# Gate and up products of a feed-forward net: one 512-column matmul for both parts of the input

## The chip, the cores and the metric

One Trainium2 chip; the program runs on 1 of its NeuronCores. The metric is the device time of one execution in microseconds (us), less is better. In the tables PE is TensorE (PEld is its loading of the stationary operand), DVE is VectorE, ACT is ScalarE, POOL is GpSimd and SP is SyncE, which here only issues DMAs.

## What is computed

Two transformer blocks, one after the other, on 256 tokens of width 1024, in float32. Between them lie six feed-forward nets of the same form (two in the first block, four in the second), two mixed attention layers, a stick-breaking attention and a sliding-window attention. Only the feed-forward nets are touched:

```python
# first block, for each of 2 layers:
h = rms_norm(x, ffn_norm[l])
x = x + (jax.nn.silu(h @ w_gate[l]) * (h @ w_up[l])) @ w_down[l]
# second block, four times:
x = x + 0.5 * swiglu(rms_norm_2(x, gain), w_gate_up, w_down)
def swiglu(h, w_gate_up, w_down):
    gate, up = jnp.split(h @ w_gate_up, 2, axis=-1)
    return (jax.nn.silu(gate) * up) @ w_down
```

The hidden width is 2816, which is 22 blocks of 128.

## The kernel before

**Float32 out of two parts.** Every operand of a large product is split into a high part, rounded to the matmul's input format, and a low part, the rest. A product is three matmuls into one PSUM region (`mm3`, lines 397 to 400): high by high (L398), then the two mixed ones (L399, L400). Low by low is left out.

**Weights.** All weights stream from HBM in units of up to 128 x 1024. SP issues a unit's DMA into one of 5 `raw` buffers; ACT copies it to the high part `wh` (L224) and DVE subtracts to get the low part `wl` (L225). There are 8 pairs of `wh` and `wl`. `free` (L246) drops a unit after its last use and calls `pump` (L242), which splits further units until 6 are alive. So a split stands in ACT's and DVE's order right behind the product that freed a unit, and ahead of whatever the program writes next. Each engine runs its instructions in the order in which they are written; the program is recorded in source order and nothing reorders it.

**A feed-forward net** (`ffn`, L499). The normed input lies transposed in `hh` and `hl` (high and low part, each 128 x 2 token tiles x 8 x 128). Hidden blocks 0 and 1 are made first, in another form with tokens as rows (two PSUM banks `gu`, two tiles `sgs` of the tag `sg`). Then the loop over f = 2 to 21 makes one hidden block each, with tokens as columns: gate into the left half of a PSUM bank (`gemm_a`, 8 steps k of three 256-column matmuls), up into the right half, then Silu (L543), the multiplication (L544), and the split into `ah` and `al` (`hilo`, L487 and L488). In each pass the down product of block f-2 follows (`rows_steps`, 12 matmuls of 512 columns into `o`), so `ah` and `al` have two passes of time. Passes 2, 20 and 21 have no down product, and pass 3 has those of blocks 0 and 1.

**Pass 3** holds one more thing: between its gate and its up product the tiles `sgs` of blocks 0 and 1 are transposed on PE into the bank `aT` (L528) and split by `hilo`; its down products need that result at the end of the same pass. The tag `sg` has two buffers, both held by `sgs` until those transposes have read them:

```python
            sg = wk.tile([128, 256], F32, name="sg", tag="sg", bufs=2)
            ACT.activation(out=sg, in_=ps[:, 0:256], func=AF.Silu)
            DVE.tensor_tensor(out=sg, in0=ps[:, 256:512], in1=sg, op=ALU.mult)
            acts[f] = act_tiles()
            hilo(sg, *acts[f])
```

So the Silu of pass 2 (and the one of pass 3) can't be written to `sg` before these transposes.

**PSUM.** `gbank` deals out four banks for `gu`, `tp` and `aT`; four others hold the down product.

Of the kernel before, what the change touches and what calls it, by code (L numbers as in the profile page):

```python
# [10 lines left out]
F32 = mybir.dt.float32  # L11
F32R = mybir.dt.float32r
BF16 = mybir.dt.bfloat16
I32 = mybir.dt.int32
AF = mybir.ActivationFunctionType
ALU = mybir.AluOpType
# [160 lines left out]
def kernel(ctx: ExitStack, tc: tile.TileContext, x_in, wst, gains, rows, pos, rpb, t5, cst_in, out):  # L177
    nc = tc.nc
    PE, ACT, DVE, POOL = nc.tensor, nc.scalar, nc.vector, nc.gpsimd

    pc = ctx.enter_context(tc.tile_pool(name="const", bufs=1))
    wk = ctx.enter_context(tc.tile_pool(name="work", bufs=2))
# [30 lines left out]
    def flush():  # L213
        while late:
            late.pop(0)()
# [14 lines left out]
    def ahead(n, engine=None):  # L230
        while done["split"] <= min(n, len(units) - 1):
            split_piece(done["split"], engine or DVE)
            done["split"] += 1

    def unit(key):
        n = index[key]
        ahead(n)
        if n + 1 == done["split"]:
            flush()
        return split[n]  # L240

    def pump():  # L242
        while not held[0] and len(split) < (W_BUFS if far[0] else LIVE) and done["split"] < len(units):
            ahead(done["split"])

    def free(key):  # L246
        del split[index[key]]
        pump()
# [2 lines left out]
    cst = pc.tile([128, C_END], F32, name="cst")  # L251
    row = pc.tile([128, R_END], F32, name="row")
    x = pc.tile([128, 2, D], F32, name="x")
    hh = pc.tile([128, 2, 8, 128], F32R, name="hh")
    hl = pc.tile([128, 2, 8, 128], F32R, name="hl")
    ident = cst[:, C_ID:C_ID + 128]
    zero = pc.tile([128, 1], F32, name="zero")
    mhalf = pc.tile([128, 8], F32, name="mhalf")
# [11 lines left out]
    def gbank(name):  # L270
        return pp.tile([128, 512], F32, name=name, tag="g", bufs=4)
# [100 lines left out]
    def posts(a, b):  # L372

        return {a: lambda: norm_post(1, (0,)), b: lambda: norm_post(1, (1,))}
# [22 lines left out]
    def mm3(ps, lh, ll, rh, rl, first, last):  # L397
        PE.matmul(ps, lhsT=lh, rhs=rh, start=first, stop=False)  # L398
        PE.matmul(ps, lhsT=ll, rhs=rh, start=False, stop=False)  # L399
        PE.matmul(ps, lhsT=lh, rhs=rl, start=False, stop=last)  # L400

    def gemm_a(key, ps):

        wh, wl = unit(key)
        for k in range(8):
            sl = slice(k * 128, (k + 1) * 128)
            mm3(ps, wh[:, sl], wl[:, sl], hh[:, :, k, :], hl[:, :, k, :], k == 0, k == 7)
            if k == 3:
                yield
        free(key)  # L410
        yield

    def gemm_b(keys, outs, n, nk, tiles=(0, 1), between=None):


        for i in tiles:
            for u, key in enumerate(keys):
                wh, wl = unit(key)
                for kk in range(nk):
                    k = u * nk + kk  # L420
                    sl = slice(kk * n, (kk + 1) * n)
                    if between and k in between:
                        between[k]()
                    mm3(outs[i], hh[:, i, k, :], hl[:, i, k, :], wh[:, sl], wl[:, sl], k == 0, k == 7)
                if i == 1:
                    free(key)
                yield
# [13 lines left out]
    def rows_steps(keys, acts, scale, nxt):  # L441


        banks = [[dbank("o") for _ in range(2)] for _ in range(2)]
        n = len(keys)

        def ready(c):
            while acts(c) is None:
                yield "wait"

        for c in range(n - SKEW):
            yield from ready(c)
            for i in range(2):
                rows_product(keys[c], *acts(c), banks, i, first=c == 0)
                yield
        far[0] = True
        pump()
        for c in range(n - SKEW, n - 1):
            yield from ready(c)
            rows_product(keys[c], *acts(c), banks, 0, halves=(0, 1) if c < n - 2 else (0,))  # L460
            yield
        yield from ready(n - 1)
        held[0] = True
        rows_product(keys[n - 1], *acts(n - 1), banks, 0, last=True, halves=(0,))
        residual(0, 0, banks, scale, nxt)
        rows_product(keys[n - 2], *acts(n - 2), banks, 0, halves=(1,))
        rows_product(keys[n - 1], *acts(n - 1), banks, 0, last=True, halves=(1,))
        yield
        residual(0, 1, banks, scale, nxt)
        finish(0, nxt)  # L470
        for c in range(n - SKEW, n - 2):
            rows_product(keys[c], *acts(c), banks, 1)
        rows_product(keys[n - 2], *acts(n - 2), banks, 1, halves=(0,))
        rows_product(keys[n - 1], *acts(n - 1), banks, 1, last=True, halves=(0,))
        residual(1, 0, banks, scale, nxt)
        if nxt is not None:
            norm_post(0)
        rows_product(keys[n - 2], *acts(n - 2), banks, 1, halves=(1,))
        rows_product(keys[n - 1], *acts(n - 1), banks, 1, last=True, halves=(1,))
        residual(1, 1, banks, scale, nxt)  # L480
        if nxt == 2:
            ahead(done["split"])
        finish(1, nxt)
        held[0] = far[0] = False

    def hilo(src, hi, lo):
        ACT.activation(out=hi, in_=src, func=AF.Copy)  # L487
        DVE.tensor_tensor(out=lo, in0=src, in1=hi.bitcast(F32), op=ALU.subtract)  # L488
# [5 lines left out]
    def drain(gen):  # L494
        for _ in gen:
            pass


    def ffn(tag, scale, nxt):  # L499
        if tag == ("ffn", 0):  # L500
            load_hank(1)
        acts = {}
        heads, sgs = [gbank("gu") for _ in range(2)], []
        for i in range(2):
            for part, c in (("g", 0), ("u", 256)):
                between = posts(T0, T1) if i == 0 and part == "u" else None
                drain(gemm_b([(tag, part, "head", j) for j in range(2)], {i: heads[i][:, c:c + 256]}, 256, 4, (i,), between))
            sg = wk.tile([128, 256], F32, name="sg", tag="sg", bufs=2)
            ACT.activation(out=sg, in_=heads[i][:, 0:256], func=AF.Silu)
            DVE.tensor_tensor(out=sg, in0=heads[i][:, 256:512], in1=sg, op=ALU.mult)  # L510
            sgs.append(sg)
            if i == 0:
                pump()
        order = [(tag, "d", f) for f in range(NF)]
        down = rows_steps(order, lambda c: acts.get(c), scale, nxt)

        def steps(n):
            for _ in range(n):
                next(down, None)

        for f in range(2, NF):
            ps = gbank("gu")
            drain(gemm_a((tag, "g", f), ps[:, 0:256]))
            if f == 3:
                pt = gbank("aT")
                for i in range(2):
                    for g in range(2):
                        PE.transpose(pt[:, g * 256 + i * 128:g * 256 + (i + 1) * 128], sgs[i][:, g * 128:(g + 1) * 128], ident)  # L528
                for g in range(2):
                    acts[g] = act_tiles()  # L530
                    hilo(pt[:, g * 256:(g + 1) * 256], *acts[g])
            if f == NF - 2:
                far[0] = True
            if f == 4 and settled:
                settle()
            if f == 6 and tag == ("ffn", 0):
                prepare_rope()
            if f == 12 and tag == ("ffn", 0):
                na_bias(1)
            held[0] = f == NF - 1  # L540
            drain(gemm_a((tag, "u", f), ps[:, 256:512]))
            sg = wk.tile([128, 256], F32, name="sg", tag="sg", bufs=2)
            ACT.activation(out=sg, in_=ps[:, 0:256], func=AF.Silu)  # L543
            DVE.tensor_tensor(out=sg, in0=ps[:, 256:512], in1=sg, op=ALU.mult)  # L544
            acts[f] = act_tiles()
            hilo(sg, *acts[f])
            held[0] = False
            pump()
            if 3 <= f < NF - 2:
                steps(4 if f == 3 else 2)  # L550
            acts.pop(f - 4, None)
        drain(down)
# [71 lines left out]
    def load_hank(l):  # L624

        hanks[l] = []
        for h in range(4):
            t = wk.tile([128, 6, 64], F32, name="hank", tag="cat", bufs=4)
            for rl in range(2):
                POOL.dma_start(out=t[rl * 64:(rl + 1) * 64],  # L630
                                  in_=bass.AP(rpb.tensor, rpb.offset + ((l * 4 + h) * 15 + 5 - rl) * 127,
                                              [[1, 64], [127, 6], [1, 64]]))
            hanks[l].append(t)
# [779 lines left out]
```

## Time and profile before

| | |
|---|---|
| three runs, median | 1611.92 us (1611.55 to 1612.4) |
| the profiled execution | 1613.55 us |
| its span, first to last instruction | 1611.8 us |
| mean granted TensorE clock | 0.998 |
| PE, PEld busy | 98%, 90% |
| DVE, ACT, POOL busy | 60%, 51%, 4% |
| matmuls of gate and up in the loop (256 columns) | 5760 |
| matmuls of the down products and output products (512 columns) | 1968 |

The profile is of one execution. The busy share of PE counts a matmul from its start to its modelled end, and matmuls overlap; what a matmul costs in a row of matmuls is the step from its start to the next one's. In the chain of waits the span is followed back from the last instruction, at each step to what released it; what stands there with a large share set the time. "Idle before" in the views of one engine is time in which it waited, with the instruction that ended the wait.

### The profile page before, as it was taken

What the parts mean: (1) busy time and instruction counts of PE and PEld (TensorE: products, weight loads), DVE (VectorE), ACT (ScalarE), POOL (GpSimd) and SP (SyncE); (2) the same over time, 40 slices, a digit from 0 to 9 for tenths busy, and PEclk for the clock granted to TensorE, in tenths of its full rate; (3) what the DMA queues carried; (4) which work ended last, traced back from release to release, by engine and by line L of the source; (5) the groups of instructions that cost most, each with busy time, mean ns of one, the idle gap of its engine ahead of it and who ended that gap; (6) DMA issues with size and microseconds to landing.
All of it is one profiled execution on the core that took longest, in us unless ns stands there. A gap on an engine that the chain in (4) does not pass through costs nothing.

```text
span 1611.8 us, 27684 instructions
## 1 busy us (share of the span) xinstructions
PE 1580.2 (98%) x11204; PEld 1452.2 (90%) x11204; DVE 965.8 (60%) x1619; ACT 819.4 (51%) x1405; POOL 59.1 (4%) x86
## 2 busy tenths in 40 slices
PE   7999999999999999999999999999999999999999
PEld 6888999988899998999999989999999998699998
DVE  6786655577665456755565466545655558865553
ACT  5665444457654444544447764444444446754442
POOL 1101000020000000000000000000000002000000
PEclk9999999999999999999999999999999999999999
DMA  8635555553355555465545437555456564246552
GB/s 268 217 122 164 199 199 194 176 170 119 106 174 194 194 195 171 172 220 182 185 146 195 133 104 242 180 192 198 168 196 195 179 189 131 83 152 203 182 183 75
DMA packets 79088, 279.99 MB, mean 174 GB/s; under 512 B 9072, under 2 KB 10608, under 8 KB 78960
## 3 DMA queue, kind: packets, MB, share of 16 engines
q1 hardware_dynamic: 78192, 276.64, 52.2%
q0 software_dynamic: 768, 1.57, 0.5%
q8 instruction: 88, 1.44, 0.3%
q14 instruction: 40, 0.33, 0.1%
HBM read 277.13 MB, written 1.05 MB: 173 GB/s over the span
## 4 chain that ended last, share of the span: by engine, by line
PE 90%; DVE 4%; ACT 2%; DMA 2%; issue 1%; SPq 0%; POOL 0%; DVEq 0%; ACTq 0%; POOLq 0%
PE gu L398 15%; PE gu L399 15%; PE gu L400 15%; PE o L399 9%; PE o L400 9%; PE o L398 9%; DVE wl L225 2%; PE s L801 2%; PE k L398 1%; DMA raw<-in_w_dram 1%; PE k L399 1%; PE k L400 1%; PE q L398 1%; PE v L398 1%; PE v L400 1%; PE q L399 1%
## 5 line engine op out<-in xcount | busy, mean ns | idle before, releaser
L225 DVE TENSOR_TENSOR wl<-raw,wh 128x1024 fp32r<-128x1024 f32 (+2 forms) x510 | 601.1, 1221 | 117.0 <-ACT wh L224 116.1
L398 PE MATMUL gu<-hh,wh 128*128 128x256 f32 x1920 | 540.2, 281 | 0.0
L400 PE MATMUL gu<-hl,wh 128*128 128x256 f32 x1920 | 539.4, 281 | 0.0
L399 PE MATMUL gu<-hh,wl 128*128 128x256 f32 x1920 | 538.9, 281 | 0.0
L224 ACT ACTIVATE wh<-raw 128x1024 fp32r<-128x1024 f32 (+2 forms) x510 | 506.5, 1042 | 50.3 <-DMA raw<-in_w_dram 30.1
L399 PEld LDWEIGHTS gu<-hh,wl 128*128 128x128 f32 x1920 | 361.8, 188 | 4.0
L398 PEld LDWEIGHTS gu<-hh,wh 128*128 128x128 f32 x1920 | 361.4, 188 | 4.0
L400 PEld LDWEIGHTS gu<-hl,wh 128*128 128x128 f32 x1920 | 361.6, 188 | 0.0
L543 ACT ACTIVATE sg<-gu 128x256 f32<-128x256 f32 x120 | 45.9, 383 | 434.9 <-PE gu L400 421.7
L399 PE MATMUL o<-wh,al 128*128 128x512 f32 x656 | 258.4, 394 | 3.9 <-DVE al L488 3.9
L398 PE MATMUL o<-wh,ah 128*128 128x512 f32 x656 | 259.9, 396 | 0.4 <-ACT ah L487 0.4
L400 PE MATMUL o<-wl,ah 128*128 128x512 f32 x656 | 257.7, 393 | 0.0
L544 DVE TENSOR_TENSOR sg<-gu,sg 128x256 f32<-128x256 f32 x120 | 50.9, 424 | 303.4 <-ACT sg L543 303.4
L399 PEld LDWEIGHTS o<-wh,al 128*128 128x128 f32 x656 | 123.2, 188 | 28.5 <-DVE al L488 6.3
L400 PEld LDWEIGHTS o<-wl,ah 128*128 128x128 f32 x656 | 123.1, 188 | 26.7
L398 PEld LDWEIGHTS o<-wh,ah 128*128 128x128 f32 x656 | 123.6, 188 | 25.7 <-issue 2.8
L488 DVE TENSOR_TENSOR al<-sg,ah 128x256 fp32r<-128x256 f32 x120 | 51.1, 426 | 58.0 <-ACT ah L487 58.0
L487 ACT ACTIVATE ah<-sg 128x256 fp32r<-128x256 f32 x120 | 50.1, 418 | 70.1 <-DVE sg L544 70.1
L616 ACT ACTIVATE p<-p,mn 128x256 f32<-128x256 f32 x96 | 46.1, 482 | 30.3 <-DVE mn L613 30.1
L487 ACT ACTIVATE hh<-tp 128x512 fp32r<-128x512 f32 x40 | 23.0, 598 | 64.0 <-PE tp L368 64.0
L398 PE MATMUL gu<-wh,hh 128*128 128x256 f32 x192 | 54.7, 285 | 0.0
L399 PE MATMUL gu<-wh,hl 128*128 128x256 f32 x192 | 54.1, 282 | 0.0
(242 smaller groups left out, 1892.8 us busy)
## 6 DMA issues: line engine op xcount, KB each, us to landing
raw<-in_w_dram SPq DMA_DIRECT2D x498, 512.0 KB, 4.6
gb<-in_gains_dram SPq DMA_DIRECT2D x11, 512.0 KB, 4.8
raw<-in_w_dram SPq DMA_DIRECT2D x8, 416.0 KB, 5.4
hank<-in_t_dram SPq DMA_DIRECT2D x8, 192.0 KB, 5.0
hank<-in_rpb_dram POOLq DMA_DIRECT2D x16, 96.0 KB, 5.1
out_dram<-x SPq DMA_DIRECT2D x4, 256.0 KB, 2.0
raw<-in_w_dram SPq DMA_DIRECT2D x2, 384.0 KB, 4.0
x<-in_x_dram SPq DMA_DIRECT2D x2, 256.0 KB, 3.0
```

Of the source, the lines that this page charges most:

```text
L224: ACT.activation(out=hi, in_=src, func=AF.Copy)
L225: late.append(lambda: engine.tensor_tensor(out=lo, in0=src, in1=hi.bitcast(F32), op=ALU.subtract))
L398: PE.matmul(ps, lhsT=lh, rhs=rh, start=first, stop=False)
L399: PE.matmul(ps, lhsT=ll, rhs=rh, start=False, stop=False)
L400: PE.matmul(ps, lhsT=lh, rhs=rl, start=False, stop=last)
L487: ACT.activation(out=hi, in_=src, func=AF.Copy)
L488: DVE.tensor_tensor(out=lo, in0=src, in1=hi.bitcast(F32), op=ALU.subtract)
L543: ACT.activation(out=sg, in_=ps[:, 0:256], func=AF.Silu)
L544: DVE.tensor_tensor(out=sg, in0=ps[:, 256:512], in1=sg, op=ALU.mult)
L616: ACT.activation(out=p[:, sl], in_=p[:, sl], func=AF.Exp, scale=-1.0, bias=mn[:, b:b + 1], accum_out=sm[:, b:b + 1])
L801: PE.matmul(ps[:, i * 256:(i + 1) * 256], lhsT=q[pr, i * 128:(i + 1) * 128], rhs=k[pr, :], start=True, stop=True)
```

## The change

`hh` and `hl` become two views of one tile `hx`, so that both parts of the input for one k can be streamed as one right-hand side of 4 x 128 columns. For the blocks 2 to 21, gate and up are made by a new function: per k one 512-column matmul by `wh` (left half of the bank: `wh` by `hh`; right half: `wh` by `hl`) and one 256-column matmul by `wl` into the left half. Gate and up now have a bank each. The halves are added afterwards by `whole`: ACT copies the right half to an SBUF tile `t`, DVE adds the left half to it. Silu is written after the gate's product and reads `t`; the multiplication reads `t` and `sg`.

```diff
-    hh = pc.tile([128, 2, 8, 128], F32R, name="hh")
-    hl = pc.tile([128, 2, 8, 128], F32R, name="hl")
+    hx = pc.tile([128, 4, 8, 128], F32R, name="hx")
+    hh, hl = hx[:, 0:2], hx[:, 2:4]
...
+    def gemm_wide(key, ps):
+        wh, wl = unit(key)
+        for k in range(8):
+            sl = slice(k * 128, (k + 1) * 128)
+            def high():
+                PE.matmul(ps, lhsT=wh[:, sl], rhs=hx[:, :, k, :], start=k == 0, stop=k == 7)
+            if k < 7:
+                high()
+            PE.matmul(ps[:, 0:256], lhsT=wl[:, sl], rhs=hh[:, :, k, :], start=False, stop=False)
+            if k == 7:
+                high()
+        free(key)
...
         for f in range(2, NF):
-            ps = gbank("gu")
-            drain(gemm_a((tag, "g", f), ps[:, 0:256]))
+            t = wk.tile([128, 512], F32, name="t", tag="p", bufs=5)
+            sg = wk.tile([128, 256], F32, name="sg", tag="sg", bufs=2)
+            def whole(ps, c):
+                ACT.activation(out=t[:, c:c + 256], in_=ps[:, 256:512], func=AF.Copy)
+                DVE.tensor_tensor(out=t[:, c:c + 256], in0=ps[:, 0:256], in1=t[:, c:c + 256], op=ALU.add)
+            ps = gbank("g")
+            gemm_wide((tag, "g", f), ps)
+            whole(ps, 0)
+            ACT.activation(out=sg, in_=t[:, 0:256], func=AF.Silu)
             if f == 3:
...
-            drain(gemm_a((tag, "u", f), ps[:, 256:512]))
-            sg = wk.tile([128, 256], F32, name="sg", tag="sg", bufs=2)
-            ACT.activation(out=sg, in_=ps[:, 0:256], func=AF.Silu)
-            DVE.tensor_tensor(out=sg, in0=ps[:, 256:512], in1=sg, op=ALU.mult)
+            ps = gbank("u")
+            gemm_wide((tag, "u", f), ps)
+            whole(ps, 256)
+            DVE.tensor_tensor(out=sg, in0=t[:, 256:512], in1=sg, op=ALU.mult)
```

The order in which ACT's instructions stand moves most at passes 2 and 3. These are ACT's instructions of the kernel before from the end of pass 2's gate to the transposed blocks, in the first feed-forward net of the second block's second layer (`sg_12790` is pass 2's Silu, `ah_12793` its high part, `ah_12833` and `ah_12837` are the high parts of the transposed blocks, `wh` are splits of weights):

```order
L224 ACTIVATE wh_12756<-raw_12666 128x1024
L224 ACTIVATE wh_12786<-raw_12684 128x1024
L543 ACTIVATE sg_12790<-gu_12729 128x256
L487 ACTIVATE ah_12793<-sg_12790 128x256
L224 ACTIVATE wh_12824<-raw_12702 128x1024
L487 ACTIVATE ah_12833<-aT_12828 128x256
L487 ACTIVATE ah_12837<-aT_12828 128x256
```

The Silu is the first of them that needs the transposes; three instructions stand between it and the second transposed half's. These are ACT's instructions of the changed kernel at the same place (`t_11928` is pass 2's sum, `t_11986` pass 3's, `g` and `u` the banks, `ah_12019` and `ah_12023` the transposed blocks):

```order
L224 ACTIVATE wh_11949<-raw_11865 128x1024
L543 ACTIVATE t_11928<-g_11930 128x256
L549 ACTIVATE sg_11929<-t_11928 128x256
L224 ACTIVATE wh_11975<-raw_11883 128x1024
L543 ACTIVATE t_11928<-u_11956 128x256
L504 ACTIVATE ah_11982<-sg_11929 128x256
L224 ACTIVATE wh_12007<-raw_11901 128x1024
L543 ACTIVATE t_11986<-g_11988 128x256
L549 ACTIVATE sg_11987<-t_11986 128x256
L504 ACTIVATE ah_12019<-aT_12014 128x256
L504 ACTIVATE ah_12023<-aT_12014 128x256
```

The Silu of pass 2 now stands ahead of the split `wh_11975` and of the copy of pass 2's up product, and the Silu of pass 3 with its copy ahead of the transposed blocks. PE's order at the same place, from the last matmuls of pass 3's gate to the first of its up product:

```order
L425 MATMUL g_11988<-hx_67,wl_11868 128x256 x2
L421 MATMUL g_11988<-hx_67,wh_11867 128x512
L554 MATMUL aT_12014<-cst_64,sg_11838 128x128 x2
L554 MATMUL aT_12014<-cst_64,sg_11925 128x128 x2
L421 MATMUL u_12027<-hx_67,wh_11903 128x512
L425 MATMUL u_12027<-hx_67,wl_11904 128x256
```

The transposes stand where they stood, between gate and up of pass 3; the products around them are now pairs of a 512-column and a 256-column matmul.

## Rows read from the trace of the kernel before

**Rows 1.** The page's first lines: span, and busy time of each engine.

```profile
span 1611.8 us, 27684 instructions
PE 1580.2 (98%) x11204; PEld 1452.2 (90%) x11204; DVE 965.8 (60%) x1619; ACT 819.4 (51%) x1405; POOL 59.1 (4%) x86
```

**Rows 2.** The chain of waits, shares of the span by engine.

```profile
PE 90%; DVE 4%; ACT 2%; DMA 2%; issue 1%; SPq 0%; POOL 0%; DVEq 0%; ACTq 0%; POOLq 0%
```

**Rows 3.** Groups of instructions: busy us, mean ns | idle before, releaser.

```profile
L225 DVE TENSOR_TENSOR wl<-raw,wh 128x1024 fp32r<-128x1024 f32 (+2 forms) x510 | 601.1, 1221 | 117.0 <-ACT wh L224 116.1
...
L224 ACT ACTIVATE wh<-raw 128x1024 fp32r<-128x1024 f32 (+2 forms) x510 | 506.5, 1042 | 50.3 <-DMA raw<-in_w_dram 30.1
...
L543 ACT ACTIVATE sg<-gu 128x256 f32<-128x256 f32 x120 | 45.9, 383 | 434.9 <-PE gu L400 421.7
...
L544 DVE TENSOR_TENSOR sg<-gu,sg 128x256 f32<-128x256 f32 x120 | 50.9, 424 | 303.4 <-ACT sg L543 303.4
...
L487 ACT ACTIVATE ah<-sg 128x256 fp32r<-128x256 f32 x120 | 50.1, 418 | 70.1 <-DVE sg L544 70.1
```

**Rows 4.** PE's instructions in time, one pass: start us, us, instruction.

```profile
694.28 0.28 PE L398 MATMUL gu<-hh,wh 128*128 128x256 f32 x1
...
699.96 0.40 PE L398 MATMUL o<-wh,ah 128*128 128x512 f32 x1
...
702.73 0.28 PE L398 MATMUL gu<-hh,wh 128*128 128x256 f32 x1
```

**Rows 5.** PE in time: the end of one net, then pass 3 of the next.

```profile
1132.06 0.40 PE L398 MATMUL o<-wh,ah 128*128 128x512 f32 x1
...
1164.60 0.60 PE L528 MATMUL aT<-cst,sg 128*128 128x128 f32 x4
...
1167.88 0.39 PE L398 MATMUL o<-wh,ah 128*128 128x512 f32 x1
1168.91 0.50 PE L399 MATMUL o<-wh,al 128*128 128x512 f32 x1 [0.65 <-DVE al L488]
```

**Rows 6.** ACT's instructions in time, in the same two nets.

```profile
1133.19 0.42 ACT L487 ACTIVATE ah<-sg 128x256 fp32r<-128x256 f32 x1 [0.49 <-DVE sg L544]
...
1150.76 0.38 ACT L509 ACTIVATE sg<-gu 128x256 f32<-128x256 f32 x1
1151.02 4.85 ACT L224 ACTIVATE wh<-raw 128x1024 fp32r<-128x1024 f32 x5
...
1165.02 0.38 ACT L543 ACTIVATE sg<-gu 128x256 f32<-128x256 f32 x1 [2.71 <-PE aT L528]
1165.89 0.42 ACT L487 ACTIVATE ah<-sg 128x256 fp32r<-128x256 f32 x1 [0.49 <-DVE sg L544]
1166.22 1.05 ACT L224 ACTIVATE wh<-raw 128x1024 fp32r<-128x1024 f32 x1
1167.17 0.36 ACT L487 ACTIVATE ah<-aT 128x256 fp32r<-128x256 f32 x1
```

**Rows 7.** DVE's instructions in time, pass 3 of the second.

```profile
1165.43 0.42 DVE L544 TENSOR_TENSOR sg<-gu,sg 128x256 f32<-128x256 f32 x1 [1.87 <-ACT sg L543]
...
1167.30 1.23 DVE L225 TENSOR_TENSOR wl<-raw,wh 128x1024 fp32r<-128x1024 f32 x1 [0.53 <-ACT wh L224]
1168.44 0.42 DVE L488 TENSOR_TENSOR al<-aT,ah 128x256 fp32r<-128x256 f32 x1
```

**Rows 8.** Stretches: length, busy us of five engines, granted clock, DMA, GB/s.

```profile
340.00:342.00 2.00, 2.00 (x11) 2.00 (x10) 1.26 (x7) 0.24 (x1) 0.60 (x1) 0.50 0.71 182
342.00:343.00 1.00, 1.00 (x4) 0.95 (x4) 1.00 (x4) 0.00 (x0) 0.76 (x1) 0.50 0.47 188
...
1360.00:1362.00 2.00, 0.00 (x0) 0.00 (x0) 1.35 (x4) 0.93 (x4) 1.84 (x4) 1.00 0.60 156
```

**Rows 9.** PE in time, ahead of the first of these stretches.

```profile
338.42 0.39 PE L398 MATMUL v<-wh,hh 128*128 128x256 f32 x1 [1.28 <-ACT wh L224]
...
339.68 0.38 PE L400 MATMUL v<-wl,hh 128*128 128x256 f32 x1 [0.76 <-DVE sw L705]
```

## The prediction, on record before the changed kernel ran

> **What bounds the kernel now.** I read the busy times first: PE is busy in 98% of the span, DVE in 60%, ACT in 51% [rows 1]. A busy PE alone proves nothing, since its matmuls overlap, so the chain of waits comes next: 90% of it is PE, 4% DVE, 2% ACT [rows 2]. The kernel ends when PE has worked through its list. A change is then worth what it takes out of that list, less what it makes PE wait. The price of a matmul is the step from start to start, not its duration. From 694.28 to 699.96 us stand the 48 matmuls of one pass's gate and up, 118.3 ns each; from 699.96 to 702.73 the 12 of a down product, 230.8 ns each [rows 4]. A pass takes 8.45 us, and PE waits for nothing in it. Last I looked for places where PE does wait in a feed-forward net, since other engines' work is free only away from those. There is one in each of the six nets, in pass 3: the second down matmul starts 1.03 us after the first instead of 0.23, held by the low part of the transposed blocks, a loss of 0.80 us [rows 5]. Behind it stands a chain that begins when the transposes release Silu's buffer. I priced that chain again for the new order.
>
> **PE's list.** Per step k, three 256-column matmuls (355.0 ns) become one of 512 and one of 256 columns (230.8 + 118.3 = 349.1 ns). The columns streamed are the same; what goes is one matmul's fixed share, 5.8 ns. A product of 8 steps saves 47 ns, and there are 240 of them. The up product of pass 3 saves nothing, as PE waits behind it; 234 x 0.0467 = **10.9 us** are left. The 512-column step is taken from the down products, whose right-hand side is one run of weights; no row shows a right-hand side of four runs of 128. The bounds are 0 (the wide matmul costs as much as two narrow ones) and 21.8 us: at 2.4 GHz, the level that the clock has in nearly all of the span, 256 columns are 106.7 ns, so that a narrow matmul has 11.6 ns beyond its columns, and at most those go with it. I take 5.8 because both steps are measured in the same pass. The Trainium skill (TensorE: Matmul & The Clock Gate, section "Wait — 56ns, not 53.3ns?") gives a warm step as columns over 2.4 GHz plus about 2.5 ns, for any width; by that the change would save 2.5 ns per step k, an estimate of 4.7 us in all. Both steps measured here are longer than that rule has them (109.2 and 215.8 ns), and the measured ones stand in the sum.
>
> **ACT and DVE in a common pass.** Added are two copies and two additions per pass. ACT has three splits, Silu and the high part, 3 x 1.04 + 0.38 + 0.42 = 3.9 us [rows 3]; two copies at about Silu's price make it 4.7 of 8.4 us. DVE goes from 3 x 1.22 + 2 x 0.42 = 4.5 to 5.4 us. A block's parts are needed two passes later, and a split is made six units ahead, so the new waits (ACT for the end of gate and of up, DVE for each copy) have cover: I cost them at nothing. If the cover went, each block would be late by the addition and the step to the next engine, some 0.5 us, or 60 us over 120 passes. The last block of a net has least cover. Its high part starts 1.13 us after the first of the 15 matmuls (3.46 us) that still need nothing of it [rows 5, 6]. The added copy, addition and a split of 0.95 us that now stands between them move it by about 1.4, which still fits. The gate's own bank costs nothing either: four banks go round, and each was added up a pass earlier.
>
> **Pass 3.** Silu of pass 2 writes a buffer that the transposes read. Before, it starts 0.42 us after they do (1164.60 to 1165.02), having held ACT for 2.71 us [rows 5, 6]; the parts of pass 2, one split and the transposed blocks follow. Now the same Silu stands ahead of a split and of pass 2's up copy, and the copy and Silu of pass 3's gate stand ahead of the transposed blocks. Everything between has to run after the transposes. From their start, each interval taken between two starts of [rows 5 to 7]:
>
> - Silu 0.42; split behind it 0.26 later (as 1150.76 to 1151.02): 0.68.
> - The split's low part on DVE 1.08 later, and DVE is free for the addition 1.14 after that (1166.22, 1167.30, 1168.44): 2.90. The up copy ended before, on ACT.
> - Multiplication and high part of block 2, 0.46 each (1165.43 to 1165.89): 3.82.
> - Next split 0.33 later: 4.15; its low part 1.08 later, the gate's addition 1.14 later: 6.37.
> - Silu of pass 3, 0.46: 6.83; high part of the transposed block 0.26: 7.09; low part 0.46: 7.55; PE starts 0.47 after that (1168.44 to 1168.91): **8.02 us**.
>
> Before, it was 1168.91 - 1164.60 = 4.31. So each net gets 3.71 us longer here, **22.3 us** for six. PE arrives after 3.28 (1164.60 to 1167.88) - 0.05 + 0.23 = 3.46 us and waits about 4.6. The second half follows within 0.9 us, under the eleven matmuls of the first, and no later wait comes of it: the splits that are late belong to pass 4 and the passes after it, and ACT and DVE have 3 us free per pass. DMAs start later with them, but five buffers lie ahead. Bounds: 0.8 us as now, and 10 us if the two splits also wait for their data.
>
> **The clock.** A wait of 4.6 us is longer than any in a feed-forward net before. After waits of 1.28 and 0.76 us close together [rows 9] the granted clock was 0.50, the 1.2 GHz level, from 340 to 343 us, while PE worked [rows 8]; half of such a stretch, 1.5 us, is lost. It stayed at 1.00 through 2 us without a matmul at 1360 [rows 8]. I expect one fall in each net and, since part of it may lie in the wait, 1.1 us for each: **6.6 us**, with bounds of 0 and 9. The Trainium skill (TensorE: Matmul & The Clock Gate, "HAM oscillation — how this bites in real kernels") also has PE's clock halved after it sat idle between bursts; the trace agrees in the one stretch and not in the other.
>
> **Sum.** -10.9 + 22.3 + 6.6 = +18.0 us. The profiled execution (1613.55 us, span 1611.8) lies 1.6 us above the median of 1611.92, so its intervals hold for the median: **1629.9 us**, 1.1% slower. With 3 to 8 ns per step, 0.6 to 1.6 us per fall and half a microsecond either way in the chain, this case runs from 1622 to 1637.
>
> **Rivals.**
>
> - *Faster:* the chain in pass 3 hardly grows. It decides at 39 x 0.0467 = 1.8 us of growth per net: if the transposed block is ready 6.1 us after the transposes, the net breaks even, below that it gains. That happens if both splits are done before Silu blocks ACT. For it: the weights are there by then. Against it: in the new order they stand behind that Silu, and ACT sat idle for 2.71 us at this place before. With the wait unchanged, 1611.9 - 11.2 = 1600.7.
> - *No fall of the clock:* for it the 2 us at 1360; 1629.9 - 6.6 = 1623.3.
> - *A narrow matmul's whole 11.6 ns go:* 1629.9 - 10.9 = 1619.0; without a fall of the clock 1612.4, no change. Against it: the 512-column step has 17.5 ns beyond its columns, more than the narrow one, so most of this share grows with the columns.
> - *The wide matmul saves nothing* (four runs in its right-hand side, or by a rule as the page's, which comes near it): 1629.9 + 10.9 = 1640.8.
> - *ACT and DVE late in every pass:* up to 60 us; against it are their 3 us free.
>
> **How the numbers follow.** Forecast 0.55, no fall 0.13, whole share saved 0.09, nothing saved 0.08, faster 0.12, late in every pass 0.03. A measurement of this kernel can tell 0.2%, 3.2 us, from no change. Faster by more than that: the rival and a little of the combinations, 0.13; within it, the whole share without a fall, 0.06; slower 0.81. The range from 1615 to 1640 leaves out the faster rival, no change and the worst, 0.2.
>
> **What would show it.** In the profile after: 256 and 512 columns alternating at 118 and 231 ns, a pass of 8.35 us; six waits of PE of 4 to 5 us on the transposed blocks in pass 3, with ACT idle until the transposes and then busy with Silu, split, copy, split, copy, Silu; a clock of 0.50 behind them; no other new wait. I am wrong if PE's wait there is about what it was, or if PE waits in common passes.

## The result, and the profile after

The changed kernel takes **1640.68 us** (median of 4 runs, 1637.25 to 1641.32) against 1612.16 (4 runs, 1611.55 to 1612.99): a ratio of 1.0174, 95% interval 1.0158 to 1.0190. It is slower, as forecast, but by 28.5 us where 18.0 were forecast, and 0.7 us beyond the upper end of the range. The profiled execution took 1640.97 us.

First the page's head, which answers to [rows 1]: span, instructions, busy time of each engine.

```profile
span 1639.2 us, 24178 instructions
PE 1587.1 (97%) x9284; PEld 1368.8 (84%) x9284; DVE 1064.3 (65%) x1859; ACT 909.7 (55%) x1645; POOL 59.0 (4%) x86
```

There are 1920 matmuls less, and DVE and ACT have 98 and 90 us more to do; the mean clock is 0.985 (before 0.998). PE's matmuls in time, for one common pass (start us, us, instruction), answer to [rows 4]:

```profile
1214.64 0.40 PE L421 MATMUL g<-hx,wh 128*128 128x512 f32 x1
1214.87 0.28 PE L425 MATMUL g<-hx,wl 128*128 128x256 f32 x1
1214.99 0.39 PE L421 MATMUL g<-hx,wh 128*128 128x512 f32 x1
...
1222.98 0.40 PE L421 MATMUL g<-hx,wh 128*128 128x512 f32 x1
```

The two widths alternate at about 230 and 118 ns from start to start, and the pass takes 8.34 us in place of 8.45. So the products did get shorter, and the loss is elsewhere. The waits of PE (what waited, for whom: us in total, times, longest) name one large place that was not on this list before:

```profile
PE o L398 <- ACT ah L504: 25.9, 6, 4.3
```

Six waits of 4.3 us, one per net. PE in time, pass 3 of the fifth net, answers to [rows 5]:

```profile
1183.17 0.60 PE L554 MATMUL aT<-cst,sg 128*128 128x128 f32 x4
...
1186.20 0.40 PE L421 MATMUL u<-hx,wh 128*128 128x512 f32 x1
1190.90 0.79 PE L398 MATMUL o<-wh,ah 128*128 128x512 f32 x1 [4.31 <-ACT ah L504]
1191.50 0.66 PE L399 MATMUL o<-wh,al 128*128 128x512 f32 x1
1191.95 0.63 PE L400 MATMUL o<-wl,ah 128*128 128x512 f32 x1
```

The second down matmul starts 8.33 us after the transposes (before 4.31), and the steps behind it are 0.43 to 0.60 us, not 0.23. The reason for the first is in ACT's order, which answers to [rows 6]:

```profile
1178.77 0.36 ACT L543 ACTIVATE t<-g 128x256 f32<-128x256 f32 x1
1183.59 0.42 ACT L549 ACTIVATE sg<-t 128x256 f32<-128x256 f32 x1 [4.46 <-PE aT L554]
1183.92 1.04 ACT L224 ACTIVATE wh<-raw 128x1024 fp32r<-128x1024 f32 x1
1184.87 0.36 ACT L543 ACTIVATE t<-u 128x256 f32<-128x256 f32 x1
1187.12 0.42 ACT L504 ACTIVATE ah<-sg 128x256 fp32r<-128x256 f32 x1 [1.89 <-DVE sg L570]
1187.44 1.04 ACT L224 ACTIVATE wh<-raw 128x1024 fp32r<-128x1024 f32 x1
1188.39 0.36 ACT L543 ACTIVATE t<-g 128x256 f32<-128x256 f32 x1
1190.16 0.42 ACT L549 ACTIVATE sg<-t 128x256 f32<-128x256 f32 x1 [1.41 <-DVE t L544]
1190.48 0.36 ACT L504 ACTIVATE ah<-aT 128x256 fp32r<-128x256 f32 x1
```

and in DVE's, which answers to [rows 7]:

```profile
1184.99 1.22 DVE L225 TENSOR_TENSOR wl<-raw,wh 128x1024 fp32r<-128x1024 f32 x1 [4.54 <-ACT wh L224]
1186.14 0.42 DVE L544 TENSOR_TENSOR t<-u,t 128x256 f32<-128x256 f32 x1
1186.66 0.43 DVE L570 TENSOR_TENSOR sg<-t,sg 128x256 f32<-128x256 f32 x1
...
1188.51 1.23 DVE L225 TENSOR_TENSOR wl<-raw,wh 128x1024 fp32r<-128x1024 f32 x1 [0.52 <-ACT wh L224]
1189.66 0.42 DVE L544 TENSOR_TENSOR t<-g,t 128x256 f32<-128x256 f32 x1
```

Read the two together, from Silu at 1183.59: split, its low part on DVE, the up addition, the multiplication, back to ACT for the high part, the next split, its low part, the gate's addition, back to ACT for the next Silu, and only then the high part of the transposed block that PE waits for. Each engine is idle while the other works. The steps of 0.43 us have their reason in the clock. The stretches (length, busy us of PE, PEld, DVE, ACT, POOL, granted clock, DMA, GB/s) answer to [rows 8]:

```profile
1186.00:1190.00 4.00, 0.59 (x4) 0.27 (x2) 2.89 (x6) 1.63 (x3) 0.00 (x0) 1.00 0.44 133
1190.00:1191.00 1.00, 0.10 (x1) 0.10 (x1) 0.19 (x2) 0.69 (x2) 0.00 (x0) 0.83 0.48 57
1191.00:1194.00 3.00, 3.00 (x7) 2.36 (x8) 2.03 (x4) 1.60 (x3) 0.00 (x0) 0.50 0.39 156
1194.00:1196.00 2.00, 2.00 (x10) 1.59 (x9) 1.12 (x3) 1.24 (x2) 0.00 (x0) 0.98 0.48 119
```

PE hardly works from 1186 to 1190 at a clock of 1.00; the clock falls as the wait ends, and the matmuls behind the wait run at 0.50, the 1.2 GHz level, until 1194. In the sixth net the wait ends at 1471.12, and the low clock lasts twice as long:

```profile
1471.00:1474.00 3.00, 2.88 (x7) 2.23 (x8) 1.93 (x3) 1.67 (x4) 0.00 (x0) 0.50 0.47 168
1474.00:1477.00 3.00, 3.00 (x9) 2.33 (x8) 1.96 (x5) 2.03 (x3) 0.00 (x0) 0.50 0.57 172
```

**Where the 27.4 us of the two spans' difference lie.** From the starts of PE's matmuls I cut every net into stretches and summed each over the six nets. A net runs from the first matmul of its first block to the first matmul of the next stage:

| stretch of a net | before, us | after, us | sum over six nets |
|---|---|---|---|
| transposes to second down matmul | 4.31 | 8.18 to 8.33 | +23.9 |
| from there to pass 4 (23 matmuls) | 5.36 to 5.39 | 6.45 to 7.90 | +11.5 |
| passes 4 to 21 (36 products) | 146.51 | 144.78 | -10.3 |
| end of the loop to the next stage | 10.70 to 12.80 | 10.66 to 14.04 | +2.7 |
| first blocks, gate of passes 2 and 3, up of 2 | | | -0.4 |
| all six nets | 1132.6 | 1160.0 | +27.4 |

Outside the nets the two differ by less than 0.1 us. The fourth row, the ends of the nets, was not in the forecast. PE loses it at two places. The first is the low part of the last hidden block, in the second to the fifth net. At the end of the fourth, where the first matmul behind the last product starts at 1150.20 (before at 1132.06 [rows 5]), PE and DVE read:

```profile
1153.65 0.49 PE L398 MATMUL o<-wh,ah 128*128 128x512 f32 x1
1154.11 0.50 PE L399 MATMUL o<-wh,al 128*128 128x512 f32 x1
1154.44 0.40 PE L400 MATMUL o<-wl,ah 128*128 128x512 f32 x1
```

```profile
1153.62 0.43 DVE L505 TENSOR_TENSOR al<-sg,ah 128x256 fp32r<-128x256 f32 x1 [0.48 <-ACT ah L504]
```

The low part is done at 1154.05, and the steps from L398 to L399 to L400 are 0.46 and 0.33 us; before, every step there is 0.23. This costs 0.38 us in each of the four nets, 1.5 us in all. The second place is the norm of the next stage, behind the residual additions on DVE. Before:

```profile
1134.59 1.23 DVE L225 TENSOR_TENSOR wl<-raw,wh 128x1024 fp32r<-128x1024 f32 x1 [0.52 <-ACT wh L224]
1136.38 0.69 DVE L389 SCALAR_TENSOR_TENSOR x<-o,x 128x512 f32<-128x512 f32 x1 [0.57 <-PE o L400]
...
1140.57 1.42 DVE L324 SCALAR_TENSOR_TENSOR xn<-x,rz,gb 128x512 f32<-128x512 f32 x2
```

and after:

```profile
1154.58 1.23 DVE L225 TENSOR_TENSOR wl<-raw,wh 128x1024 fp32r<-128x1024 f32 x1 [0.53 <-ACT wh L224]
1155.72 1.28 DVE L389 SCALAR_TENSOR_TENSOR x<-o,x 128x512 f32<-128x512 f32 x2
...
1159.14 1.42 DVE L324 SCALAR_TENSOR_TENSOR xn<-x,rz,gb 128x512 f32<-128x512 f32 x2
```

The freed weight's split stands in DVE's order between the last block and the residual additions. It starts 4.38 us after the first matmul behind the last product (before 2.53), so the first addition, which had waited for PE and started at +4.32, starts at +5.52, and the norm of the next stage at +8.94 for +8.51. PE pays 0.1 us for that in the third to the fifth net, and 0.9 us in the second, where it waits 1.43 us for the normed input (before 0.53).

### The profile page after: what moved, and what is told of

Same layout as the page of the kernel before. It is cut to its first block, busy times and chain, and to the rows that moved or that the text cites. A ratio compares the mean times of both kernels' runs of the same rounds, so it can differ in the third digit from the quotient of the medians.

```text
span 1639.2 us, 24178 instructions
## 1 busy us (share of the span) xinstructions
PE 1587.1 (97%) x9284; PEld 1368.8 (84%) x9284; DVE 1064.3 (65%) x1859; ACT 909.7 (55%) x1645; POOL 59.0 (4%) x86
## 4 chain that ended last, share of the span: by engine, by line
PE 89%; DVE 4%; ACT 3%; issue 2%; DMA 2%; POOL 0%; SPq 0%; DVEq 0%; ACTq 0%; POOLq 0%
PE g L421 13%; PE u L421 13%; PE o L398 9%; PE o L399 9%; PE o L400 9%; PE g L425 7%; PE u L425 6%; DVE wl L225 2%; PE s L827 1%; ACT wh L224 1%; PE gu L399 1%; PE gu L400 1%; PE gu L398 1%; DMA raw<-in_w_dram 1%; PE k L398 1%
## 5 line engine op out<-in xcount | busy, mean ns | idle before, releaser
L421 PE MATMUL u<-hx,wh 128*128 128x512 f32 x960 | 348.2, 396 | 0.0
L421 PE MATMUL g<-hx,wh 128*128 128x512 f32 x960 | 345.0, 393 | 0.0
L398 PE MATMUL o<-wh,ah 128*128 128x512 f32 x656 | 268.7, 410 | 25.9 <-ACT ah L504 25.9
L399 PE MATMUL o<-wh,al 128*128 128x512 f32 x656 | 263.5, 402 | 0.0
L400 PE MATMUL o<-wl,ah 128*128 128x512 f32 x656 | 261.2, 398 | 0.0
L425 PE MATMUL u<-hx,wl 128*128 128x256 f32 x960 | 249.8, 281 | 0.0
L425 PE MATMUL g<-hx,wl 128*128 128x256 f32 x960 | 249.3, 280 | 0.0
L421 PEld LDWEIGHTS g<-hx,wh 128*128 128x128 f32 x960 | 180.3, 188 | 35.0
L421 PEld LDWEIGHTS u<-hx,wh 128*128 128x128 f32 x960 | 180.4, 188 | 32.8
L425 PEld LDWEIGHTS u<-hx,wl 128*128 128x128 f32 x960 | 181.1, 189 | 10.1
L425 PEld LDWEIGHTS g<-hx,wl 128*128 128x128 f32 x960 | 180.6, 188 | 9.7
L398 PEld LDWEIGHTS o<-wh,ah 128*128 128x128 f32 x656 | 126.9, 193 | 55.2 <-ACT ah L504 29.0
L399 PEld LDWEIGHTS o<-wh,al 128*128 128x128 f32 x656 | 126.8, 193 | 28.4 <-DVE al L505 2.5
L400 PEld LDWEIGHTS o<-wl,ah 128*128 128x128 f32 x656 | 126.6, 193 | 28.4
L549 ACT ACTIVATE sg<-t 128x256 f32<-128x256 f32 x120 | 50.1, 418 | 93.6 <-DVE t L544 72.0
L544 DVE TENSOR_TENSOR t<-g,t 128x256 f32<-128x256 f32 x120 | 50.8, 423 | 74.8 <-ACT t L543 74.8
```

The source lines that it names most:

```text
L421: PE.matmul(ps, lhsT=wh[:, sl], rhs=hx[:, :, k, :], start=k == 0, stop=k == 7)
L425: PE.matmul(ps[:, 0:256], lhsT=wl[:, sl], rhs=hh[:, :, k, :], start=False, stop=False)
L544: DVE.tensor_tensor(out=t[:, c:c + 256], in0=ps[:, 0:256], in1=t[:, c:c + 256], op=ALU.add)
L549: ACT.activation(out=sg, in_=t[:, 0:256], func=AF.Silu)
```

## The experiments

Each kernel was timed beside the kernel before (1611.5 to 1612.3 us in these comparisons). The theory had three links: Silu of pass 2 waits for its buffer; the copies, additions and splits then run one after the other; the long wait costs clock.

**Four buffers for Silu's result.** Both tiles of the tag `sg` in `ffn`, in the changed kernel:

```diff
-sg = wk.tile([128, 256], F32, name="sg", tag="sg", bufs=2)
+sg = wk.tile([128, 256], F32, name="sg", tag="sg", bufs=4)
```

> The changed kernel with four buffers for the tag sg instead of two, so that the Silu of passes 2 and 3 need not wait for the transposes. Theory of the order (ACT stands still at that Silu, and what is written behind it runs late): PE's wait in pass 3 goes altogether, also the 0.80 us of the kernel before, and no clock of 0.50 follows it; 240 products x 48 ns = 11.5 us and 6 x 0.80 = 4.8 us below the kernel before, some 2.7 us given back at the nets' ends: about 1598.6 us. Rival, the added copies and additions are themselves too much for ACT and DVE in pass 3: PE still waits 2 us or more there, 1612 us or over.

Measured: 1618.34 us (1617.58 to 1620.14), ratio 1.0041 (1.0026 to 1.0056). A miss by 20 us: the buffer was 22 us of the loss, and not the whole. The transposes-to-first-matmul stretch is 4.30 to 6.57 us in the six nets (7.73 with two buffers, 3.28 before). In its fifth net the transposes start at 1168.29; ACT and DVE in time:

```profile
1166.33 0.42 ACT L549 ACTIVATE sg<-t 128x256 f32<-128x256 f32 x1 [1.36 <-DVE t L544]
...
1167.60 0.36 ACT L543 ACTIVATE t<-u 128x256 f32<-128x256 f32 x1
...
1172.77 0.42 ACT L549 ACTIVATE sg<-t 128x256 f32<-128x256 f32 x1 [1.36 <-DVE t L544]
1173.09 0.36 ACT L504 ACTIVATE ah<-aT 128x256 fp32r<-128x256 f32 x1
```

```profile
1171.18 1.22 DVE L225 TENSOR_TENSOR wl<-raw,wh 128x1024 fp32r<-128x1024 f32 x1 [0.52 <-ACT wh L224]
1172.32 0.42 DVE L544 TENSOR_TENSOR t<-g,t 128x256 f32<-128x256 f32 x1
```

Silu now runs ahead of the transposes; that wait is gone. But both Silus shown still wait 1.36 us for their addition, which stands behind a split of 1.22 us on DVE, and ACT does nothing that is written after them. That is the second link, and it needs no lack of a buffer. It has a fixed length: in all six nets the first down matmul starts 5.91 to 5.92 us after the copy of pass 2's up product (here at 1167.60), and that copy starts between 1.62 us ahead of the transposes and 0.66 us behind them. What moves the copy was not tried.

**The same four buffers in the kernel before.**

> The kernel before with four buffers for sg, as a control. Theory of the order: its six waits of 0.80 us come from the same release, and go: 1612.2 - 4.8 = 1607.4 us. Rival, they come from ACT's and DVE's work in pass 3: no change, 1612.

Measured: 1607.45 us (1606.34 to 1608.49), ratio 0.9971 (0.9960 to 0.9982), and 0.23 to 0.41 us between the two down matmuls, as expected. The buffer is worth 4.9 us without the change and 22.3 us with it: the change raised the price of a wait that was there already.

**Silu written behind the second addition**, with two buffers as in the change:

```diff
             whole(ps, 0)
-            ACT.activation(out=sg, in_=t[:, 0:256], func=AF.Silu)
...
             whole(ps, 256)
+            ACT.activation(out=sg, in_=t[:, 0:256], func=AF.Silu)
```

> The changed kernel with one instruction moved: Silu is written after the up product's copy and addition instead of after the gate's. Same work, two sg buffers. Theory of the order: split, up copy and up addition of pass 2 now run ahead of the transposes; the second down matmul comes 4.8 us after the transposes (before 4.3, after 8.3), the clock does not fall: about 1606 us. Rival, the work itself: 1635 us or over.

Measured: 1605.87 us (1602.64 to 1608.89), ratio 0.9962 (0.9951 to 0.9972): 34.8 us less than the change, and faster than before. Same matmuls, same copies and additions; one instruction stands elsewhere. PE in its fifth net:

```profile
1156.12 0.60 PE L553 MATMUL aT<-cst,sg 128*128 128x128 f32 x4
...
1159.41 0.50 PE L398 MATMUL o<-wh,ah 128*128 128x512 f32 x1
1160.79 0.50 PE L399 MATMUL o<-wh,al 128*128 128x512 f32 x1 [0.88 <-DVE al L505]
```

The first down matmul is back at 3.29 us, without a wait (3.52 in the fourth net). The second still waits 0.88 us, so that 0.36 us of the loss is left per net (4.67 us after the transposes, 4.31 before; 4.90 in the fourth net). The stretch behind it is back at 5.34 to 5.39 us in all six nets. The ends of the nets come back too (11.89 in the middle nets, before 11.86), though the same split is still there, on DVE at the end of the fourth net:

```profile
1126.72 1.23 DVE L225 TENSOR_TENSOR wl<-raw,wh 128x1024 fp32r<-128x1024 f32 x1 [0.52 <-ACT wh L224]
1127.89 0.69 DVE L389 SCALAR_TENSOR_TENSOR x<-o,x 128x512 f32<-128x512 f32 x1
1129.25 0.69 DVE L389 SCALAR_TENSOR_TENSOR x<-o,x 128x512 f32<-128x512 f32 x1 [0.67 <-PE o L400]
```

The first matmul after the last product starts at 1123.60 here, so the split is at +3.12 and the second addition waits for PE again, at +5.65 (before +5.68). The last block's high part starts at +1.72 (+2.97 in the change), and PE loses no step to it.

**The clock by itself.** Sixteen throwaway matmuls into a spare bank, where PE waits in pass 3:

```diff
             gemm_wide((tag, "u", f), ps)
+            if f == 3:
+                idle = gbank("idle")
+                for z in range(16):
+                    PE.matmul(idle, lhsT=hh[:, 0, z % 8, :], rhs=hx[:, :, z % 8, :], start=z == 0, stop=z == 15)
             whole(ps, 256)
```

> The changed kernel with 16 extra 512-column matmuls (3.7 us, into a spare bank, read by nobody) between the up product and the down products of pass 3, where PE waits. Theory that the slow matmuls behind the wait are the clock's fall, and that the fall comes of the wait: the wait's end stays where it is (7.7 us after the transposes), the clock stays at 1.00 and the 23 steps from the second down matmul to pass 4 take 5.3 us again instead of 6.4 to 7.9: 11.5 us less, about 1629 us. Rival, they are slow by contention with the splits that catch up: no gain, 1640 us.

Measured: 1627.65 us (1626.69 to 1629.12), 13.0 us under the change, with more work on PE. In its fifth net:

```profile
1176.57 3.92 PE L572 MATMUL idle<-hx 128*128 128x512 f32 x16
1180.87 0.49 PE L398 MATMUL o<-wh,ah 128*128 128x512 f32 x1 [0.38 <-ACT ah L504]
1181.33 0.50 PE L399 MATMUL o<-wh,al 128*128 128x512 f32 x1
```

```profile
1178.00:1182.00 4.00, 3.62 (x15) 2.48 (x15) 2.26 (x4) 2.10 (x6) 0.00 (x0) 1.00 0.47 169
1182.00:1186.00 4.00, 4.00 (x20) 3.28 (x18) 2.56 (x5) 2.19 (x5) 0.00 (x0) 1.00 0.36 114
```

The chain is as long as in the change (7.74 us to the first down matmul in each net), the clock stays at 1.00 in these stretches, and the stretch behind is at 5.33 to 5.35 us. In the two profiled executions the nets sum to 12.1 us less than in the change: that is the price of six falls of the clock. Another 1.6 us lies between the first and the second net (see the last section).

**The wide form from pass 4 on.** `gemm_wide`, copies and additions only for `f >= 4`, passes 2 and 3 in the form before:

```diff
+            wide = f >= 4
...
+            else:
+                drain(gemm_a((tag, "g", f), ps[:, 0:256]))
```

> The wide form only in passes 4 to 21; passes 2 and 3 keep the old products, the old accumulator bank and the old order of Silu. Theory (the loss sits in pass 3: a serial chain between ScalarE and VectorE of copy, addition, Silu and split, and behind its 4.3 us wait a low clock): pass 3 is as in the kernel before (3.3 and 1.0 us around the first down matmul, 5.4 us for the steps behind it, no stretch at 0.50 there), each of 36 x 6 products saves 48 ns (10.4 us), and the last blocks still lose 2.7 us per run: 1612.3 - 10.4 + 2.7 = 1604.6 us. Rival (the copies and additions cost time in every pass): the passes 4 to 21 are not shorter by 48 ns per product, and the time is 1612 us or more.

Measured: 1605.94 us (1604.92 to 1607.57), ratio 0.9963 (0.9950 to 0.9976). Pass 3 is as before (3.28 and 1.03 us), passes 4 to 21 take 144.78 us, and the ends still cost 2.8 us. So the wide products are worth their 10.3 us where nothing waits.

**The wide form in passes 4 to 19**, with `wide = 4 <= f < NF - 2` in the same place:

> As the kernel with the wide form from pass 4 on, and the last two passes, 20 and 21, in the old form too. Theory (the end of a net is late because the last block's split waits behind copy, addition and Silu): the stretch from the last block to the next stage is back at the 11.8 to 11.9 us of the kernel before in the middle nets, and with 32 x 6 products at 48 ns (9.2 us) the time is 1612.3 - 9.2 = 1603.1 us, 1.5 us under the kernel with the wide form in 20 and 21 (2.7 us of tails against 1.2 us of products). Rival (the end is late because of something that the wide products leave behind, such as the residual additions' own queue): the ends stay at 12.3 us, and the time is 1605.8 us.

Measured: 1603.70 us (1602.34 to 1605.24), ratio 0.9949 (0.9935 to 0.9962). The middle nets' ends are at 11.92 us, and the second net's at 12.87 (14.04 in the change). The loss at the ends belongs to the last block's copies, additions and Silu. The intervals of these two kernels overlap, so their times alone don't tell them apart; the stretches do.

**Both: Silu late and four buffers.**

> Both parts at once: Silu issued behind the second copy and addition, and four buffers for the gate value in place of two. With the order alone the time was 1605.9 us, with 3.3 us from the transposes to the first down matmul and 1.38 us from there to the second; with the buffers alone it was 1618.3 us, with 0.46 us there. Theory (two separate links: the order makes ScalarE wait for VectorE in every pass, the buffers make pass 2's Silu wait for the transposes): both go, the first stretch stays at 3.3 us and the second falls to 0.4 us: 1605.9 - 6 x 1.0 = 1600 us. Rival (four buffers let Silu start early and put ScalarE back to waiting for VectorE's additions): the first stretch grows past 3.3 us as it did with the buffers alone, and the time is 1606 us or more.

Measured: 1602.26 us (1599.0 to 1603.83), ratio 0.9935 (0.9923 to 0.9948). The first stretch stays at 3.25 to 3.42 us, against the rival. But the second fell to 0.23 us in two nets only; it is 0.86 and 0.91 in two, and 1.38 and 1.39 in the first and the last. In the last net ACT waited 0.97, 1.09 and 0.77 us for the weights' DMA in front of three splits, and pass 2's up copy came 0.79 us ahead of the transposes, where in the fifth it came 2.62 us ahead. In the four nets with a wait the second down matmul starts 5.60 to 5.63 us after that copy, whenever it came; in the other two the copy came 2.62 us ahead of the transposes, and PE does not wait. So the start of the copy sets what is left. The trace points to late weights as what delays it; that was not tried by itself.

**All together:** wide from pass 4 on, Silu late, four buffers.

> All that the runs so far taught in one kernel: old products in passes 2 and 3, the wide form from pass 4 on with Silu issued behind the second copy and addition, four buffers for the gate value. Theory (the parts add up): the kernel before with four buffers took 1607.4 us; 36 x 6 products at 48 ns give 10.4 us; the late Silu keeps the last block's split early, so that the ends of the nets stay at 11.9 us: 1607.4 - 10.4 = 1597.0 us. Rival (four buffers with wide passes behind bring ScalarE's waits on VectorE back into pass 3): no better than the wide form everywhere with the same order and buffers, 1602 us.

Measured: 1598.69 us (1596.65 to 1601.82), ratio 0.9925 (0.9912 to 0.9939), the fastest median. The second down matmul follows the first after 0.23 to 0.37 us in all nets; the nets sum to 1117.2 us, 15.4 under the kernel before. The interval overlaps that of the last experiment, with the wide form in every pass (0.9923 to 0.9948), so which of the two is better isn't settled by their times; both beat the two kernels of this study.

## Why the prediction was right, and where it was wrong

Direction and mechanism were right; the time was too low, mainly by two terms, the fall of the clock and the ends of the nets.

| term | forecast, us | measured, us |
|---|---|---|
| products | -10.9 | -10.7 |
| chain in pass 3, at full clock | +22.3 | +23.3 |
| fall of the clock | +6.6 | +12.1 |
| ends of the nets | 0 | +2.7 |
| sum | +18.0 | +27.4 |

- **Products: right.** 1.72 us over 36 products is 48 ns each (forecast 47): 10.3 us in passes 4 to 21, and 0.4 in passes 2 and 3. Four runs of 128 in the right-hand side cost nothing beside one run, so that rival falls. The Trainium skill's fixed 2.5 ns per matmul (TensorE: Matmul & The Clock Gate, section "Wait — 56ns, not 53.3ns?") is not borne out in this kernel: a merged pair gave back 6.0 ns.
- **Chain in pass 3: right in mechanism and nearly in size.** The order of the steps is the forecast one. With the clock held up the second down matmul starts 8.20 us after the transposes (8.02 forecast, 4.31 before), which is 3.89 x 6 = 23.3 us. The high part of the transposed block came at 7.31 (7.09 forecast). What I had not seen is that the *first* down matmul now waits for it, not the second for the low part.
- **Fall of the clock: the step that failed most.** I took "one fall in each net and ... 1.1 us for each", with a bound of 9 us in all. There was one fall in each net, but the matmuls from the second down matmul to pass 4 lost 1.1 to 2.5 us, 11.5 in all, and the step ahead of them 0.6; holding the clock up by throwaway matmuls gave the same 12.1 back. The price came from one stretch of 3 us [rows 8], halved and cut for what might lie in the wait. Here the clock was at 0.50 for some 3 us in the first and the fifth net and for some 7 us in the other four, of which 2.4 at most lay in the wait. By the Trainium skill (TensorE: Matmul & The Clock Gate, section "HAM oscillation — how this bites in real kernels") PE comes back at half its clock after it sat idle between bursts; the trace agrees in all six nets, but not behind every wait of the runs (last section).
- **Ends of the nets: costed at nothing, measured 2.7 us.** The sentence "move it by about 1.4, which still fits" failed on PE itself. The last block's high part came 1.84 us later, mostly because Silu stood ahead of the up copy on ACT and waited 1.36 us for an addition behind a split (1.25 us of the 1.84 go when Silu is written late); the copy, addition and split that the sentence names add up to about 1.75 us by its own prices (0.38, 0.42 and 0.95). The high part cost PE only 0.04 us, but the sentence didn't price the low part, which comes 0.45 us after it: 1.5 us in four nets. It also didn't ask what is queued behind the late work on DVE: the freed weight's split, and behind it the residual additions that the next stage needs, 1.2 us.
- **Common passes: right.** 8.34 us (8.35 forecast), no wait.

The range held the forecast case with small errors in each term; two errors of one sign, 5.5 us in the clock and 2.7 at the ends, went through its upper end. That the rival in which the wide matmul saves nothing gave 1640.8 us, 0.1 from the measured time, is chance: its condition did not hold, since the products saved 10.7 us. The chances were also added up loosely: that rival's 1640.8 lies above 1640 too, so with its 0.08 the range left out some 0.29, not 0.2, and the 1600.7 of the faster rival counts all 240 products where the sum counts 234.

The cause beneath is an order, not the added work. The run with Silu moved has every added copy and addition and little of the loss, 0.36 us per net. Writing Silu ahead of the up product put an instruction with two late inputs (a buffer that frees at the transposes, an addition behind a split) at the head of an engine that runs in order.

## What to carry to other kernels

When an added step puts a second engine between an accumulator and its reader, write the reader as late as its result is needed: behind an instruction that waits, every later copy and split waits too, and the other engine with it. A wait of PE can be priced twice, once for itself and once for the low clock behind it, which here was half as much again (23.3 and 12.1 us). Where a late block "still fits" for PE, price its low part as well as its high part, and follow it on the other engine to the last thing queued behind it.

## What was not expected of the hardware

- Throwaway matmuls paid: 16 of 512 columns per net, 3.9 us of PE's idle time each net, took 13.0 us off.
- The same wait of 4.3 us cost 1.1 us of clock in the fifth net and 2.5 in the sixth. With four buffers alone, PE arrived some 3.4 us after the transposes and so waited about 3.1, 2.4, 0.8, 2.0, 1.8 and 2.2 us in the six nets; the stretch behind was longer by 1.6 us in the first, second and fifth, and not at all in the others, though the fifth's wait is shorter than the fourth's and sixth's. The length of the wait alone doesn't tell whether the clock falls; what else decides was not tried.
- Between the first and the second net, which the change doesn't touch, the profiled executions take either 125.2 or 126.8 us: the longer time wherever the clock fell there, as at 340 us before [rows 8], the shorter where it stayed at 1.00, as in the run with throwaway matmuls. With 1.6 us of this kind, differences of a few us between two medians are better read from the stretches.
- The nine executions of the kernel with Silu late spread from 1602.64 to 1608.89 us, at mean clocks of 0.999 to 0.996, and the profiled one was the fastest. Its stretches, and those of the two kernels with Silu late and four buffers, whose profiled executions were the fastest of theirs too, show these kernels at their best; where the others lost clock, no trace shows.
